# One ones-matmul for eight squares, and two float32 gate matmuls side by side, in a two-layer mLSTM / GLA trunk

## The chip, the cores and the metric

One Trainium2 chip, all 8 cores, each with one batch element and no exchange between cores. Engines are named as the profile names them: PE multiplies matrices (PEld is its loading of weights), DVE and POOL do elementwise work, ACT activation functions. PE writes its results into PSUM, which this kernel uses as a ring of banks: a bank is free again once another engine has read ("evicted") it. The metric is the device time of the slowest core in microseconds. A program on all cores has a second, slower state: in some executions one die or both run at a lower granted clock, the share of full speed at which PE is let run (here 1535 to 1802 us). A ratio is the mean time of one kernel's fast runs over that of the other's of the same rounds, so it is not quite the ratio of the medians quoted.

## The reference, cut to what matters

```python
def rmsnorm(x, g):                       # before each mixer, each MLP, and at the end
    y = x * lax.rsqrt(jnp.mean(x * x, axis=-1, keepdims=True) + EPS)
    return y * g
# layer 1 (GLA): low-rank gate, rank 16, 4 heads x 128
z = (z_low @ w_gate_up) + b_gate         # z_low: [S,16], w_gate_up: [16,512]
log_a = jax.nn.log_sigmoid(z) / 16.0     # then a running sum over the chunk
```

The rest (projections, chunkwise mixers, squared-ReLU MLPs) is large bf16 matmuls. mLSTM (a matrix memory) and GLA (gated linear attention) are the two layers' mixers, both worked out chunk by chunk.

## The kernel before

Activations lie transposed: features on partitions, 512 tokens (a group) along the free axis. A recording layer collects operations in source order and a list scheduler with estimated durations fixes each engine's order; the estimates (`ns=`) matter for nothing else. Names that return in the profiles: xT is the residual stream, xn its normalised copy, zl the rank-16 projection, sqb the summed squares, R the mixer's running state; wqk, wv, wo, wout, w1b and w2b are weights. The RMS statistics need a sum over 1024 features: ACT squares eight tiles, POOL adds them in two halves of four, and two matmuls with a matrix of ones sum the halves over the partitions.

```python
    def sq_half(g, hf):
        ks = [hf * 4 + i for i in range(4)]
        for i, k in enumerate(ks):
            act(sq[:, i % 2, :], xT[:, k, tgs(g)], AF.Square, ...)
            if i == 1:   tt(sd, sq[:, 0], sq[:, 1], ALU.add, ..., "pool")
            elif i == 2: tt(sd, sd, sq[:, 0], ALU.add, ..., "pool")
            elif i == 3: tt(sqb[:, hf, :], sd, sq[:, 1], ALU.add, ..., "pool")
    def sq_sum():
        a = nb()                                        # a PSUM bank of the ring
        for hf in range(2):
            mm(PB[a][:], ones_bf[:], sqb[:, hf, :], ...)
        rstd_fin(a)                                     # Ln, Exp on ACT through sd
```

In the GLA layer each group of tokens needs four gates, one for each head:

```python
        def zl_F(s, g):        # 8 matmuls, 16 output rows, then a copy to zl[0:16]
            ...
        def z_F(s, g, h):
            a, gp, p = nb(), g % 2, h % 2
            mm(PB[a][:], wgu[:, h * DK:(h + 1) * DK], zl[0:16, :], ..., 512, True)      # float32
            act(sd[:], PB[a][:], AF.Exp, ...)
            act(sd[:], sd[:], AF.Ln, ...)
            for c in range(4):                          # DVE: running sums, sd -> NB[p]
                tensor_tensor_scan(out=NB[:, p, chunk c], data0=ones_bf, data1=sd[:, chunk c], ...)
            act(EB[:, p, :], NB[:, p, :], AF.Exp, ..., scale=-1.0 / 16.0)
            act(NB[:, p, :], NB[:, p, :], AF.Exp, ..., scale=1.0 / 16.0)
            ...
```

(… marks cuts.)

## Time and profile before

| | before |
|---|---|
| median of the first 6 runs | 1519.9 us (1519.02 to 1573.5) |
| spans of the 8 cores, profiled run | 1512.3 to 1518.3 us |
| matmuls on PE | 7,554 (144 records are missing on two of the cores, the slowest among them) |
| PE busy / DVE / ACT / POOL | 96% / 53% / 40% / 12% |

A matmul's record lasts longer than the time after which the next may start, so durations of PE overlap. What counts is the distance between starts: 216 ns for 512 bf16 columns at the full clock. The lines themselves stand in the prediction.

### The profile page before, as it was taken

Reading aid. Unit: us, or ns where it says so; the run is one execution under the profiler, and the core shown is the slowest. Engines: PE = TensorE matmul, PEld = TensorE weight load, DVE = VectorE, ACT = ScalarE, POOL = GpSimd, SP = SyncE. Lnnn points to the kernel's source line nnn. Section 1 sums busy time; section 2 is a strip of 40 time slices with the busy share of each in tenths; the row PEclk is TensorE's granted clock in tenths of the full one; section 3 lists DMA queues with packets and bytes.
Section 4 is the critical chain, followed back from the end, with each engine's and each line's share of the span. In section 5 each row is a group of like instructions: output and inputs, shape, how many; then the busy total and the mean of one; then the engine's idle time right before and its main releaser. Section 6 shows DMA issues by size and latency. Waiting matters only on the chain.

```text
span 1518.3 us, 22604 instructions; the slowest of 8 cores (1512.3 to 1518.3 us)
## 1 busy us (share of the span) xinstructions
PE 1459.6 (96%) x7410; PEld 695.1 (46%) x7554; DVE 808.2 (53%) x1449; ACT 604.9 (40%) x1255; POOL 180.9 (12%) x170
## 2 busy tenths in 40 slices
PE   5999999899999999999999999999999999999996
PEld 1555455444444444444434544444444444444444
DVE  3187474865434434434656776769643343443467
ACT  3587676642022022033345776766310310301333
POOL 3012111330000000002010202024200000000042
PEclk9999999999999999999989999999999999999999
DMA  9840003633132033033001200037330231100014
GB/s 190 173 140 1 1 2 56 91 50 53 30 56 45 12 57 56 0 56 56 1 0 37 76 1 1 1 56 112 56 56 13 43 56 29 28 1 1 1 56 167
DMA packets 37378, 72.89 MB, mean 48 GB/s; under 512 B 4480, under 2 KB 6528, under 8 KB 37264
## 3 DMA queue, kind: packets, MB, share of 16 engines
q0 software_dynamic: 28640, 58.77, 21.4%
q1 hardware_dynamic: 8624, 12.66, 2.5%
q8 instruction: 63, 1.03, 0.3%
q14 instruction: 51, 0.42, 0.1%
HBM read 109.23 MB, written 8.39 MB: 77 GB/s over the span
## 4 chain that ended last, share of the span: by engine, by line
PE 86%; DVE 5%; issue 3%; DMA 2%; ACT 2%; POOL 1%; DVEq 0%; SPq 0%; ACTq 0%; POOLq 0%
PE ps L235 86%; DVE oT L249 1%; DVE R L249 1%; DVE xT L245 1%; DMA wqk<-m_win 1%; DMA xT<-xT 1%; DVE xn L249 1%; PE ps L749 1%; DMA wst<-m_wout 0%; POOL sd L245 0%; DVE hn L249 0%; ACT sq L241 0%; DVE ps L245 0%; POOL sqb L245 0%; ACT og L241 0%
## 5 line engine op out<-in xcount | busy, mean ns | idle before, releaser
L235 PE MATMUL ps<-xn,w1b 128*128 128x512 bf16 x2006 | 442.6, 379 | 2.8 <-DVE xT L245 0.5
L235 PE MATMUL ps<-hid,w2b 128*128 128x512 bf16 (+1 forms) x1948 | 415.7, 372 | 2.9 <-DVE xT L245 0.9
L241 ACT ACTIVATE rt<-ps 128x512 f32<-128x512 f32 x256 | 152.8, 597 | 606.2 <-PE ps L235 598.9
L245 DVE TENSOR_TENSOR xT<-ps,xT 128x512 f32<-128x512 f32 (+1 forms) x328 | 219.9, 675 | 250.3 <-PE ps L235 249.2
L235 PEld LDWEIGHTS ps<-xn,w1b 128*128 128x128 bf16 x2048 | 200.1, 98 | 241.6 <-issue 1.8
L235 PEld LDWEIGHTS ps<-hid,w2b 128*128 128x128 bf16 x1984 | 193.8, 98 | 222.2 <-issue 1.8
L245 DVE TENSOR_TENSOR hid<-rt 128x512 bf16<-128x512 f32 x240 | 170.1, 711 | 222.0 <-ACT rt L241 222.0
L241 ACT ACTIVATE sq<-xT 128x512 f32<-128x512 f32 (+2 forms) x168 | 97.3, 603 | 91.1 <-DVE xT L245 44.4
L235 PE MATMUL ps<-xn,wqk 128*128 128x512 bf16 x499 | 116.3, 384 | 6.9 <-DMA wqk<-m_win 6.2
L235 PE MATMUL ps<-wo,xn 128*128 128x512 bf16 x494 | 120.0, 386 | 1.7 <-DVE xT L245 0.6
L235 PE MATMUL ps<-wv,xn 128*128 128x512 bf16 x497 | 117.7, 383 | 1.1 <-DVE og L245 0.2
L235 PE MATMUL ps<-hnT,wout 128*128 128x512 bf16 x499 | 114.3, 379 | 1.3 <-ACT sd L241 0.6
L249 DVE SCALAR_TENSOR_TENSOR xn<-xT,gains,rstd 128x512 bf16<-128x512 f32 x128 | 99.9, 821 | 21.3 <-ACT rstd L241 21.3
L245 POOL TENSOR_TENSOR sd<-sq 128x512 f32<-128x512 f32 x34 | 44.2, 1300 | 516.1 <-ACT sq L241 323.7
L241 ACT ACTIVATE og<-og 128x512 f32<-128x512 f32 x128 | 80.5, 629 | 10.5 <-ACT og L241 0.4
L235 PEld LDWEIGHTS ps<-xn,wqk 128*128 128x128 bf16 x512 | 50.1, 99 | 65.6 <-issue 9.4
L235 PEld LDWEIGHTS ps<-wv,xn 128*128 128x128 bf16 x512 | 49.4, 99 | 60.8 <-issue 7.7
L235 PEld LDWEIGHTS ps<-wo,xn 128*128 128x128 bf16 x512 | 49.7, 99 | 54.4 <-issue 6.0
L235 PEld LDWEIGHTS ps<-hnT,wout 128*128 128x128 bf16 x512 | 48.6, 98 | 56.0 <-issue 2.8
L249 DVE SCALAR_TENSOR_TENSOR R<-R,egs,ps 128x256 f32<-128x256 f32 x120 | 57.3, 478 | 11.2 <-PE ps L235 4.2
L241 ACT ACTIVATE junk<-ps 128x256 bf16<-128x256 f32 x128 | 48.7, 380 | 14.7 <-PE ps L235 5.0
L245 POOL TENSOR_TENSOR sd<-sd,sq 128x512 f32<-128x512 f32 x34 | 44.8, 1317 | 71.2 <-ACT sq L241 70.9
(121 smaller groups left out, 991.1 us busy)
## 6 DMA issues: line engine op xcount, KB each, us to landing
w1b<-w POOLq DMA_DIRECT2D x16, 1024.0 KB, 15.0
w2b<-w POOLq DMA_DIRECT2D x16, 1024.0 KB, 12.2
outT<-oT SPq DMA_DIRECT2D x12, 512.0 KB, 2.9
xT<-xT POOLq DMA_DIRECT2D x2, 2048.0 KB, 29.0
wst<-m_wout POOLq DMA_DIRECT2D x4, 1024.0 KB, 6.5
wst<-g_wout POOLq DMA_DIRECT2D x4, 1024.0 KB, 5.3
xT<-xT SPq DMA_DIRECT2D x4, 512.0 KB, 6.6
xT<-xT SPq DMA_DIRECT2D x2, 1024.0 KB, 12.5
```

Of the source, the lines that this page charges most:

```text
L235: t.op("pe", lambda e: e.matmul(out, lhsT=lhsT, rhs=rhs, start=start, stop=stop), r=r, w=w, sig=sig, ns=max(cols, 150) * (1.7 if f32 else ...
L241: t.op("act", lambda e: e.activation(out=out, in_=in_, func=func, **kw), r=r, w=w, ns=190 + 0.84 * n + (190 if acc is not None else 0))
L245: t.op(eng, lambda e: e.tensor_tensor(out=out, in0=in0, in1=in1, op=op), r=r, w=w, ns=170 + 1.03 * n if eng == "dve" else 200 + 2.2 * n)
L249: t.op("dve", lambda e: e.scalar_tensor_tensor(out=out, in0=in0, scalar=scalar, in1=in1, op0=op0, op1=op1), r=r, w=w, ns=200 + 1.07 * n)
L749: t.op("pe", lambda e, h=h, e2=e2, e8=e8: e.transpose(tpS[:, e8, :], in_=hn[:, h, e2 * 128:(e2 + 1) * 128], identity=ident[:]), r=[("hn", ...
```

## The change

The intent is to take matmuls off the tensor engine. All eight squares are added on POOL before a single ones-matmul (in 14 of 17 sums; the three at the end, where the sum is waited for, keep two). And two heads' gates are computed by two matmuls in different 32-row groups of the array: a second copy of the low-rank projection (columns 32 to 47 of a widened `wz`, zeros between) puts `zl` on partitions 32 to 47 too, where the second head's weights lie.

```diff
     def sq_half(g, hf):
+        for i in range(4):
+            k = hf * 4 + i
+            act(sq[:, i % 2, :], xT[:, k, tgs(g)], AF.Square, ...)
+            if k == 5:
+                t.op("pool", ... sd = sd + sq[:, 0] ..., ns=0, more=True)
+                tt(sd[:], sd[:], sq[:, 1, :], ALU.add, ..., "pool")
+            ...
+            elif k == 7:
+                tt(sqb[:, 0, :], sd[:], sq[:, 1, :], ALU.add, ..., "pool")
...
-    wgu, _ = at("wgu", [16, 512], F32)
-    wz, _ = at("wz", [128, KC, 16], BF16)
+    wgu, _ = at("wgu", [48, 2, 128], F32)
+    wz, _ = at("wz", [128, KC, 48], BF16)
...
-        def z_F(s, g, h):
-            mm(PB[a][:], wgu[:, h * DK:(h + 1) * DK], zl[0:16, :], ...)
-            act(sd[:], PB[a][:], AF.Exp, ...)   # and Ln; scan sd -> NB
+        def z_F(s, g, hp):
+            gp, banks = g % 2, [nb(), nb()]
+            for p in range(2):
+                mm(PB[banks[p]][:], wgu[32 * p:32 * p + 16, hp, :], zl[32 * p:32 * p + 16, :], ...,
+                   True, True, p == 1, 256, True)
+            for p in range(2):                  # Exp, Ln, scans in place in NB[p]; EB, NB as before
...
-                return qk(0) + s.z(g + 1, 2) + o + qk(1) + s.z(g + 1, 3) + ops + qk(2) + v + qk(3)
+                return qk(0) + qk(1) + s.z(g + 1, 1) + o + ops + v + qk(2) + qk(3)
```

More of the change, by code (lines that the diff above doesn't have):

```diff
@@ L56, in ov, with op @@
         return r
-    def op(s, ename, fn, r=(), w=(), ns=200, sig=True):
+    def op(s, ename, fn, r=(), w=(), ns=200, sig=True, more=False):
         reads = [k for k in r if k[0] != "B"]
@@ L69, in op @@
         u["ns"] += ns
-        if sig:
+        if sig and not more:
             s.units.append(u)
@@ L403, in load_z @@
         n = 8 if layer == 0 else 16
-        t.dma("pool", [(wz[:, :, 0:n], src[:, :, 3072:3072 + n])], 500000, r=after, w=[("wz",)])
+        t.dma("pool", [(wz[:, :, c:c + n], src[:, :, 3072:3072 + n]) for c in ((0,) if layer == 0 else (0, 32))],
+              500000, r=after, w=[("wz",)])
     def load_w1(layer, q):
@@ L437, in sq_half, with sq_half2 @@
     def sq_half(g, hf):
+        for i in range(4):
+            k = hf * 4 + i
+            act(sq[:, i % 2, :], xT[:, k, tgs(g)], AF.Square, [("xT", k, g)], [("sq", i % 2)], 512)
+            if k == 5:
+                t.op("pool", lambda e: e.tensor_tensor(out=sd[:], in0=sd[:], in1=sq[:, 0, :], op=ALU.add),
+                     r=[("sd",), ("sq", 0)], w=[("sd",)], ns=0, more=True)
+                tt(sd[:], sd[:], sq[:, 1, :], ALU.add, [("sd",), ("sq", 1)], [("sd",)], 512, "pool")
+            elif i == 1:
+                tt(sd[:], sq[:, 0, :], sq[:, 1, :], ALU.add, [("sq", 0), ("sq", 1)], [("sd",)], 512, "pool")
+            elif i == 2:
+                tt(sd[:], sd[:], sq[:, 0, :], ALU.add, [("sd",), ("sq", 0)], [("sd",)], 512, "pool")
+            elif k == 3:
+                tt(sd[:], sd[:], sq[:, 1, :], ALU.add, [("sd",), ("sq", 1)], [("sd",), ("sqb", 0)], 512, "pool")
+            elif k == 7:
+                tt(sqb[:, 0, :], sd[:], sq[:, 1, :], ALU.add, [("sd",), ("sq", 1)], [("sqb", 1)], 512, "pool")
+    def sq_half2(g, hf):
         ks = [hf * 4 + i for i in range(4)]
@@ L450, in rstd_fin, with sq_sum @@
         act(rstd[:], sd[:], AF.Exp, [("sd",)], [("rstd",)], 512, scale=-0.5)
-    def sq_sum():
+    def sq_sum(two=False):
         a = nb()
-        for hf in range(2):
-            mm(PB[a][:], ones_bf[:], sqb[:, hf, :], [("sqb", hf), ("ones_bf",)], [("B", a)], hf == 0, hf == 1,
-               hf == 1, 512)
+        if two:
+            for hf in range(2):
+                mm(PB[a][:], ones_bf[:], sqb[:, hf, :], [("sqb", hf), ("ones_bf",)], [("B", a)], hf == 0, hf == 1,
+                   hf == 1, 512)
+        else:
+            mm(PB[a][:], ones_bf[:], sqb[:, 0, :], [("sqb", 0), ("sqb", 1), ("ones_bf",)], [("B", a)], True, True,
+               True, 1024)
         rstd_fin(a)
@@ L600, in zl_F @@
             for k in range(KC):
-                mm(PB[a][0:16, :], wz[:, k, 0:16], XN[:, x, k, :], [("wz",), ("xn", x, k)], [("B", a)],
+                mm(PB[a][0:48, :], wz[:, k, :], XN[:, x, k, :], [("wz",), ("xn", x, k)], [("B", a)],
                    k == 0, k == KC - 1, k == KC - 1, 512)
-            t.op("dve", lambda e: e.tensor_copy(out=zl[0:16, :], in_=PB[a][0:16, :]), r=[("B", a)], w=[("zl",)],
+            t.op("dve", lambda e: e.tensor_copy(out=zl[0:48, :], in_=PB[a][0:48, :]), r=[("B", a)], w=[("zl",)],
@@ L604, in zl_F @@
                  ns=670)
-        def z_F(s, g, h):
-            a, gp, p = nb(), g % 2, h % 2
-            mm(PB[a][:], wgu[:, h * DK:(h + 1) * DK], zl[0:16, :], [("wgu",), ("zl",)], [("B", a)], True, True, True,
-               512, True)
-            act(sd[:], PB[a][:], AF.Exp, [("B", a), ("ngbg",)], [("sd",)], 580, scale=-1.0, bias=ngbg[:, h:h + 1])
-            act(sd[:], sd[:], AF.Ln, [("sd",)], [("sd",)], 512, bias=1.0)
-            for c in range(4):
-                t.op("dve", lambda e, c=c: e.tensor_tensor_scan(
-                    out=NB[:, p, c * CH:(c + 1) * CH], data0=ones_bf[:], data1=sd[:, c * CH:(c + 1) * CH],
-                    initial=0.0, op0=ALU.mult, op1=ALU.add), r=[("ones_bf",), ("sd",)], w=[("NB", p)], ns=425)
-            act(EB[:, p, :], NB[:, p, :], AF.Exp, [("NB", p)], [("EB", p)], 512, scale=-1.0 / 16.0)
-            act(NB[:, p, :], NB[:, p, :], AF.Exp, [("NB", p)], [("NB", p)], 512, scale=1.0 / 16.0)
-            t.op("dve", lambda e: e.tensor_copy(
-                out=egs[:, gp, h * 4:(h + 1) * 4],
-                in_=EB[:, p, :].rearrange("p (c n) -> p c n", n=CH)[:, :, CH - 1]),
-                r=[("EB", p)], w=[("egs", gp)], ns=170)
+        def z_F(s, g, hp):
+            gp, banks = g % 2, [nb(), nb()]
+            for p in range(2):
+                mm(PB[banks[p]][:], wgu[32 * p:32 * p + 16, hp, :], zl[32 * p:32 * p + 16, :], [("wgu",), ("zl",)],
+                   [("B", banks[p])], True, True, p == 1, 256, True)
+            for p in range(2):
+                h, a = hp * 2 + p, banks[p]
+                nbv, nk = NB[:, p, :], ("NB", p)
+                act(nbv, PB[a][:], AF.Exp, [("B", a), ("ngbg",)], [nk], 580, scale=-1.0, bias=ngbg[:, h:h + 1])
+                act(nbv, nbv, AF.Ln, [nk], [nk], 512, bias=1.0)
+                for c in range(4):
+                    cv = NB[:, p, c * CH:(c + 1) * CH]
+                    t.op("dve", lambda e, cv=cv: e.tensor_tensor_scan(
+                        out=cv, data0=ones_bf[:], data1=cv, initial=0.0, op0=ALU.mult, op1=ALU.add),
+                        r=[("ones_bf",), nk], w=[nk], ns=425)
+                act(EB[:, p, :], nbv, AF.Exp, [nk], [("EB", p)], 512, scale=-1.0 / 16.0)
+                act(nbv, nbv, AF.Exp, [nk], [nk], 512, scale=1.0 / 16.0)
+                t.op("dve", lambda e, h=h, p=p: e.tensor_copy(
+                    out=egs[:, gp, h * 4:(h + 1) * 4],
+                    in_=EB[:, p, :].rearrange("p (c n) -> p c n", n=CH)[:, :, CH - 1]),
+                    r=[("EB", p)], w=[("egs", gp)], ns=170)
@@ L764, in op_, with z @@
             return [lambda j=j: s.op_F(g, j) for j in range(KC)]
-        def z(s, g, h):
-            return [] if s.m else [lambda: s.z_F(g, h)]
+        def z(s, g, hp):
+            return [] if s.m else [lambda: s.z_F(g, hp)]
         def gate_slots(s, g):
@@ L788, in fills @@
                         return o + qk(3)
-                    return x[:2] + o + qk(0) + s.z(1, 2) + x[2:] + qk(1) + s.z(1, 3) + v
+                    return x[:2] + o + qk(0) + qk(1) + s.z(1, 1) + x[2:] + v
                 if c == 2:
@@ L814, in run @@
                                 addx(0, fn)
-                            for h in range(2):
-                                for fn in s.z(1, h):
-                                    addx(2, fn)
+                            for fn in s.z(1, 0):
+                                addx(2, fn)
                     elif c == 0:
@@ L826, in run @@
                             addx(n, fn)
-                        for h in range(2):
-                            for fn in s.z(g + 1, h):
-                                addx(4 + h, fn)
+                        for fn in s.z(g + 1, 0):
+                            addx(4, fn)
                 for n, fn in hooks.get(i, []):
@@ L870, in build @@
     t.dma("sp", [(ong[:], ong_d)], 1000, w=[("ong",)])
-    t.dma("sp", [(wgu[:], g_wgu_d)], 1000, w=[("wgu",)])
+    wgu_v = g_wgu_d.rearrange("r (a b n) -> r b a n", b=2, n=128)
+    t.dma("sp", [(wgu[32 * b:32 * b + 16, :, :], wgu_v[:, b]) for b in range(2)], 1000, w=[("wgu",)])
     t.dma("sp", [(gbg[:], g_bg_d)], 1000, w=[("gbg",)])
     t.op("dve", lambda e: e.memset(ones_bf[:], 1.0), w=[("ones_bf",)])
+    t.op("dve", lambda e: e.memset(wz[:], 0.0), w=[("wz",)])
     t.op("dve", lambda e: e.memset(ident[:], 0.0), w=[("ident",)])
@@ L1027, in build @@
     dn[2][0]()
+    dn[2][1]()
     m1.zl_F(0)
-    dn[2][1]()
+    dn[2][2]()
     m1.z_F(0, 0)
-    m1.z_F(0, 1)
-    dn[2][2]()
     dn[2][3]()
@@ L1036, in build @@
             fn()
-        if h < 2:
-            m1.z_F(0, 2 + h)
-            dn[2][4 + 2 * h]()
-            dn[2][5 + 2 * h]()
+        if h == 1:
+            m1.z_F(0, 1)
+            for j in range(4, 8):
+                dn[2][j]()
     for fn in m1.v(0):
@@ L1074, in build @@
             if j in (4, 7):
-                sq_half(g, j // 7)
+                sq_half2(g, j // 7)
             if gen is not None and j >= 3:
                 next(gen, None)
-        sq_sum()
+        sq_sum(True)
         gen = out_ops(g, 0, GS)
```

## The prediction

> **What bounds the kernel now.** I read the page of the slowest core first: the busy shares, the chain that ended last, the row of the granted clock. Then the waits of the tensor engine, then the two groups of matmuls that the change touches, and last their neighbourhood in the timeline.
>
> ```profile
> PE 1459.6 (96%) x7410; PEld 695.1 (46%) x7554; DVE 808.2 (53%) x1449; ACT 604.9 (40%) x1255; POOL 180.9 (12%) x170
> ...
> PE 86%; DVE 5%; issue 3%; DMA 2%; ACT 2%; POOL 1%; DVEq 0%; SPq 0%; ACTq 0%; POOLq 0%
> ```
>
> PE is busy 96% of the span and is 86% of the chain. A busy PE is not a PE at its peak, so I looked at what it waits for:
>
> ```profile
> PE ps L235 <- ACT sq L241: 16.4, 9, 8.7
> PE ps L235 <- DMA wqk<-m_win: 6.2, 1, 6.2
> PE ps L235 <- DVE R L249: 5.6, 10, 1.8
> ...
> PE ps L235 <- ACT sd L241: 0.6, 1, 0.6
> PE ps L235 <- POOL sqb L245: 0.4, 1, 0.4
> ```
>
> About 44 us in all. The first 16.4 us lie in the start-up statistics and in the last half group (both keep their code) and 6.2 us in the first weight load. The two producers in question, POOL's sqb and the statistics' Ln (sd), keep PE for 1.0 us. So almost anywhere in the two places that change, PE time taken away is time taken off the end, and PE time saved does not fall behind another wait. The question is how much PE time goes.
>
> ```profile
> L235 PE MATMUL ps<-zl,wgu 16*128 16x512 f32 x32 | 19.1, 691 | 0.0
> ...
> L235 PE MATMUL ps<-sqb,ones_bf 128*128 128x512 bf16 x33 | 10.4, 378 | 1.0 <-POOL sqb L245 0.4 <-DVE xT L245 0.4
> L245 POOL TENSOR_TENSOR sd<-sq 128x512 f32<-128x512 f32 x34 | 44.2, 1300 | 516.1 <-ACT sq L241 323.7
> ```
>
> 16 float32 gate matmuls stand as 32 records: each is two passes. The durations overlap, so I don't use them; I use distances between starts. Here is one gate matmul between two bf16 streams, and one sum of squares:
>
> ```profile
> 751.02 0.81 PE L235 MATMUL ps<-xn,wqk 128*128 128x512 bf16 x3
> 751.76 1.12 PE L235 MATMUL ps<-zl,wgu 16*128 16x512 f32 x2
> 752.82 0.61 PE L235 MATMUL ps<-xn,w2b 128*128 128x512 bf16 x2
> ...
> 774.65 0.59 PE L235 MATMUL ps<-sqb,ones_bf 128*128 128x512 bf16 x2
> ```
>
> In the single records the last bf16 matmul starts 309 ns before the gate (216 between bf16 matmuls, so 93 to get in), the two passes are 535 ns apart, and the next bf16 matmul starts 518 ns after the second: 93 + 1053 = 1146 ns for one gate. Two gates back to back (at 736.48) have passes 429 ns apart and take 93 + 1912 = 2005 ns. The two sqb matmuls are 216 ns apart.
>
> One place is odd:
>
> ```profile
> 780.00:800.00 20.00, 16.92 (x41) 5.29 (x40) 11.96 (x24) 6.22 (x12) 0.00 (x0) 0.66 0.00 0
> ```
>
> Between 780 and 800 us the granted clock is 0.66: the zl matmuls come one by one behind DVE's xn, 663 ns apart, and from 787 us all matmuls take double time for some 10 us. A gate pair falls into it and takes 3710 ns in place of 1912.
>
> **What the Trainium skill says.** "TensorE: Matmul & The Clock Gate", Single matmul / Back-to-back issue gap: a warm 512-column matmul costs 512/2.4 + 2.5, about 216 ns; this trace has 215 and 216. The same page, Part 3 (Packing small matmuls): a matmul with few contraction rows costs as much as one with 128; matmuls in different 32-row groups run at once, four of them measured 3.07 times as fast; but matmuls start and end strictly in program order, only weight loads are pulled ahead. The trace of before has only one row group in use, so it can't show the overlap; that 16 rows cost no less than 128 it does show (429 ns a pass, at float32's half rate). "TensorEngine Tiling (Array Packing)", Key Properties: a change of tiling mode drains the engine; the 93 ns into a gate and some 90 ns after its last pass (518 against 429) agree. "GPSIMD Engine Reference", section 3: a two-input elementwise op is about twice as slow as on VectorE; here 1.27 us against 0.68.
>
> **The change, part by part.**
>
> (1) Sum of squares. Of 17 sums, 14 go from two ones-matmuls to one; the three of the tail keep two. PE saves 14 x 0.216 = 3.0 us. POOL gets 7 adds a sum for 6: 14 x 1.27 = 18 us more on an engine that is 12% busy. Does the sum land later? In the second half POOL now can start when the first new square is there, and does four adds; before, it waited for two squares and did three. At 121 us, the tightest case (PE takes the sum 0.1 us before its record ends), the halves go: half one ends 121.07, square 4 is ready at 121.14, so four adds from 121.24 with no buffer wait end near 126.4; before they ended at 126.87. At 306 us the same working gives about 310 in place of 311.49, because square 4 had been ready at 300.75. Of the 14, ten have 3 us or more of slack. So the extra add costs nothing or almost nothing: 0 to 0.5 us.
>
> (2) The gates. 16 single gate matmuls become 8 pairs; the second of a pair has its weights and its zl on partitions 32 to 47, so it sits in another row group. Before, on PE: 14 runs (12 singles, two doubles, one of these cold). From the single records, start to start less 216 for the bf16 matmul ahead, they sum to 19.6 us. For a pair the program order is A pass 1, A pass 2, B pass 1, B pass 2. If order is strict and a pass must wait for the pass in its own row group, only A2 and B1 overlap: three pass times, not four and not two: 93 + 535 + 429 + 520 = 1577 ns. Seven warm pairs are 11.0 us; the one in the cold stretch was 4055 with its entry, less one cold pass of 854, 3.2 us. Sum 14.2, saving 19.6 - 14.2 = 5.4 us.
>
> (3) zl. 48 stationary columns in place of 16, 512 moving columns either way: 8 matmuls of 216 ns four times, no change; the copy to zl works on 48 partitions in the same 0.67 us. The zeros between are a memset at the start, before PE begins. The second 16-column load at 538 us puts about 0.9 us more of issue on POOL ahead of weights that are used 200 us later: hidden.
>
> (4) Exp, Ln and scan now work in place in NB, not through the one sd. The second head's Exp no longer waits for the first head's scan; the work is the same. In exchange each pair needs two PSUM banks at once of a ring of four, and both EB and NB buffers free, so the queries and keys of two heads are projected ahead of it. PE's order shows 16 to 32 other matmuls between a pair and the projections that need it, at least 7 us, against about 7 us for the pair's chain (0.69 + 0.63 + 2.0 + 1.3, the second head some 2 us later). I book 0, with 2 us either way, and another 2 us for the scheduler's other reorderings.
>
> Sum: 3.0 + 5.4 = 8.4 us off, 1519.9 - 8.4 = about **1511.5 us**, 0.55%.
>
> **The rivals.**
>
> A: full overlap, both gates in the time of one. Pair 1146 ns, seven are 8.0, the cold one about 2.35: 10.4, saving 9.2, time about 1507.5. For it: the skill's 3.07 for four tiles. Against it: that is for single-pass tiles; here the two passes of A stand together in the order.
>
> C: no overlap (the float32 passes exclude one another). Pair 2005 ns, 14.0 + 4.06 = 18.1, saving 1.5 only, from fewer entries; time about 1515.5. Nothing in this trace speaks against it.
>
> D: a new wait takes it back: PE at the ones-matmul for POOL's later sum, or PE for banks held by the gates' Exp. In the worst case four tight sums lose 1.3 us each and eight pairs 0.5 us: about 9 us, so a time as before, 1520. Slacks and the working in (1) speak against.
>
> E: the cold stretch at 787 us goes, or another comes. It is worth some 5 us at half speed plus about 4 us of waits. The order of zl, wo and the pair there is the same as before and the xn ops still pace it, so I expect it to stay; it is present on six of eight cores before.
>
> **Range and chances.** I weigh the overlap of two passes 0.5, full overlap 0.25, none 0.25; with reordering of 3 us and the cores' own spread (1512.3 to 1518.3) the range is **1504.5 to 1517.5**. 2% is 30 us; the whole work removed or at stake is 10 to 15 us, so: faster by over 2% 0.01, within 2% 0.98, slower by over 2% 0.01.
>
> **What would show it.** Ones-matmuls of sqb: 20 in place of 34, each 216 ns. Start to start from the bf16 matmul before a gate pair to the one after it, less 216: 1.58 us if two passes overlap, 1.15 if all do, 2.0 if none. The second and third pass of a pair starting within 20 ns of each other would be the overlap itself. Waits of PE for sqb and for sd stay under 2 us; POOL's busy time rises by 18 us. I am wrong if PE waits for sqb or for the gates' Exp by several us, if the chunk after a pair waits for EB or NB, or if the clock of 0.66 near 790 us is gone or has a twin elsewhere.

## The result, and the profile after

| | before | after |
|---|---|---|
| time | 1519.9 us (first session) | 1509.6 us, median of 8 runs, two of them slow (1784 us) |
| ratio of fast runs | | 0.9926, interval 0.9914 to 0.9938 |
| spans of the cores, profiled run | 1512.3 to 1518.3 us | 1500.6 to 1508.7 us |

The ratio is 11.2 us of 1519.9, where 8.4 had been forecast. The first line of the page of the kernel after (busy us, share, instructions of each engine):

```profile
PE 1446.2 (96%) x7396; PEld 691.5 (46%) x7540; DVE 810.4 (54%) x1450; ACT 604.8 (40%) x1255; POOL 199.9 (13%) x185
```

Its waits of PE, from the list of waits (total us, times, longest):

```profile
PE ps L235 <- DVE R L249: 5.5, 10, 1.1
...
PE ps L235 <- DVE xT L245: 4.6, 6, 1.3
...
PE ps L235 <- ACT ktok L241: 1.3, 1, 1.3
PE ps L235 <- POOL sqb L245: 0.8, 2, 0.6
```

PE holds 14 matmuls fewer and is 13.4 us less busy; POOL is 19.0 us busier. PE still hardly waits for the sum (0.8 us), but it waits for DVE's xT, the eviction of a PSUM bank, 4.6 us where it had been 2.4 (these are the slowest cores, core 0 before and core 6 after). Next the groups of instructions that the change touches:

```profile
L235 PE MATMUL ps<-xn,wz 128*48 128x512 bf16 x32 | 9.4, 400 | 2.2 <-DVE xn L249 2.1
L235 PE MATMUL ps<-zl,wgu 16*128 16x512 f32 x32 | 9.2, 654 | 0.0
...
L235 PE MATMUL ps<-sqb,ones_bf 128*128 128x512 bf16 x19 | 7.3, 391 | 1.4 <-POOL sqb L245 0.8 <-DVE xT L245 0.4
```

And one gate pair in the timeline of PE (start, duration, instruction, count):

```profile
745.50 0.38 PE L235 MATMUL ps<-xn,wqk 128*128 128x512 bf16 x1
745.81 1.13 PE L235 MATMUL ps<-zl,wgu 16*128 16x512 f32 x4
746.87 0.60 PE L235 MATMUL ps<-xn,w2b 128*128 128x512 bf16 x2
```

The reader sees 32 gate records as before, but 9.2 us of busy time for 19.1, and four of them between 745.81 and 746.87: two gates now take the 1.06 us that one took. 48 output rows cost zl next to nothing: eight zl matmuls that follow one another take 1.53 us from first to last start for 1.51 (the 9.4 us for 9.1 of busy time are durations, which also depend on the clock). The single records of this pair start at 0, 7, 533 and 540 ns.

To see where the time went, I added up the distances between starts of PE's records, core by core, and split them: the gates (from the bf16 matmul ahead to the one after, less 216 ns), the ones-matmuls of sqb, idle time of PE (without its longest wait, some 9 us for the first squares at the start; so the column is below the 43.5 us that the list of waits of before adds up to), and what 512-column bf16 matmuls spaced 400 to 450 ns take above 216 (half clock). Means of the six cores whose trace has all records, in us:

| kernel | span | gates | sums | PE waits | half clock | all else |
|---|---|---|---|---|---|---|
| before | 1514.2 | 19.1 | 8.3 | 31.6 | 5.7 | 1449.5 |
| after | 1504.7 | 9.7 | 4.9 | 35.4 | 4.9 | 1449.8 |
| difference | -9.5 | -9.4 | -3.4 | +3.8 | -0.8 | +0.3 |

So the change saves 12.8 us of PE's work and gives 3.8 back as waits, all of it in the second layer (7.9 to 11.6). These are one execution's mean cores; the slowest core, which the times measure, gained 9.6 in these two executions and 11 over the runs.

### The profile page after: what moved, and what is told of

Same layout as the page of the kernel before. It is cut to its first block, busy times and chain, and to the rows that moved or that the text cites. A ratio compares the mean times of both kernels' runs of the same rounds, so it can differ in the third digit from the quotient of the medians.

```text
span 1508.7 us, 22612 instructions; the slowest of 8 cores (1500.6 to 1508.7 us)
## 1 busy us (share of the span) xinstructions
PE 1446.2 (96%) x7396; PEld 691.5 (46%) x7540; DVE 810.4 (54%) x1450; ACT 604.8 (40%) x1255; POOL 199.9 (13%) x185
## 4 chain that ended last, share of the span: by engine, by line
PE 85%; DVE 7%; issue 3%; DMA 2%; ACT 2%; POOL 0%; DVEq 0%; SPq 0%; ACTq 0%; POOLq 0%
PE ps L235 84%; DVE xn L249 1%; DVE oT L249 1%; DVE R L249 1%; DMA xT<-xT 1%; DVE xT L245 1%; DMA wqk<-m_win 1%; DVE hn L249 1%; PE ps L777 1%; DMA wst<-m_wout 0%; PE ps L666 0%; DVE ps L245 0%; DMA wst<-g_wout 0%; DVE NB L641 0%; ACT og L241 0%
## 5 line engine op out<-in xcount | busy, mean ns | idle before, releaser
L245 POOL TENSOR_TENSOR sd<-sd,sq 128x512 f32<-128x512 f32 x62 | 81.2, 1310 | 73.2 <-ACT sq L241 66.7
L245 POOL TENSOR_TENSOR sd<-sq 128x512 f32<-128x512 f32 x20 | 25.9, 1295 | 466.3 <-ACT sq L241 441.0
```

Of the source, the lines that this page charges most:

```text
L245: t.op(eng, lambda e: e.tensor_tensor(out=out, in0=in0, in1=in1, op=op), r=r, w=w, ns=170 + 1.03 * n if eng == "dve" else 200 + 2.2 * n)
```

## The experiments

Theory: the pairing pays through overlap of *both* float32 passes, and the sum through the matmuls left out; some of it comes back as waits that the new order makes. Rivals: the overlap is only partial and the order or the clock brought the rest; POOL's longer sum is waited for. Eleven runs were made, nine of edited kernels and two repeats (e_after, e_late_again), all correct. The table has their split, in the columns of above.

| kernel | median, us | ratio to before, interval | gates | sums | PE waits | half clock |
|---|---|---|---|---|---|---|
| e_sq | 1516.3 | 0.9968, 0.9955 to 0.9981 | 18.4 | 4.9 | 32.1 | 4.8 |
| e_gates | 1512.2 | 0.9947, 0.9933 to 0.9960 | 9.9 | 8.5 | 34.3 | 4.3 |
| e_same_rows | 1520.2 | 0.9996, 0.9982 to 1.0009 | 17.3 | 4.9 | 37.0 | 5.4 |
| e_sig | fast runs 1509.4, 1510.1 | 0.9935, 0.9907 to 0.9962 | 9.7 | 4.9 | 35.2 | 3.7 |
| e_quad | 1512.7 | 0.9952, 0.9924 to 0.9979 | 6.0 | 4.9 | 38.1 | 6.1 |
| e_pool8 | 1519.1 | 0.9992, 0.9970 to 1.0015 | 10.4 | 4.7 | 43.2 | 6.0 |
| e_split | 1518.9 | 0.9984, 0.9971 to 0.9998 | 11.3 | 5.1 | 39.0 | 7.7 |
| e_late | 1503.3 | 0.9891, 0.9870 to 0.9912 | 9.3 | 5.0 | 33.6 | 2.9 |
| e_before_late | 1511.3 | 0.9938, 0.9918 to 0.9958 | 17.6 | 8.3 | 29.6 | 3.4 |
| e_after | 1510.7 | 0.9935, 0.9915 to 0.9956 | 9.6 | 5.0 | 36.5 | 4.9 |
| e_late_again | fast runs 1502.7 to 1503.1 | 0.9887, 0.9864 to 0.9910 | 9.2 | 4.9 | 33.9 | 2.3 |

Each ratio is against runs of the kernel before on the same chip. Medians can hold slow runs; the ratios don't.

### e_sq: the sums alone

The kernel before with the new `sq_half` and `sq_sum`, nothing else.

> The kernel before with the sum-of-squares part alone (14 of 17 sums with one ones-matmul, seven adds on POOL). Theory: PE time saved goes straight to the end and the extra add lies in slack, so 14 x 0.216 = 3.0 us plus a few tenths of transitions: 1516.2 to 1517, ratio about 0.998. PE waits for sqb under 1.5 us in all, POOL busy +18 us. Rival: POOL's later sum is waited for at the four tight sums and gives 1 to 3 us back: 1517.5 to 1520.

Measured: 0.9968, 4.9 us, with an interval of 2.9 to 6.8. The sums take 3.4 us less on PE (14 matmuls, 0.24 us each with their transitions), and waits rise by only 0.5. The theory stands; the 1 us or so above it lies in the half-clock column (-0.9), which varies from run to run, and inside the interval. With e_gates below, the two parts alone sum to 13.0 us where both together gave 11.2; the intervals are wide enough for that.

### e_gates: the pairing alone, with names

```diff
-    wgu, _ = at("wgu", [48, 2, 128], F32)
+    wgu, WG = at("wgu", [48, 2, 128], F32)
+    wguB, _ = at("wguB", [48, 2, 128], F32, WG)        # same place, a name of its own
...
-                mm(PB[banks[p]][:], wgu[32 * p:32 * p + 16, hp, :], ...)
+                mm(PB[banks[p]][:], (wguB if p else wgu)[32 * p:32 * p + 16, hp, :], ...)
```

> The gate pairing alone on the kernel before (sums of squares as before), with the second head's weights under a name of their own (wguB, same place) so that records of the two matmuls can be told apart. Theory: both float32 passes of the second head overlap those of the first, i.e. its first pass overtakes the first head's second pass: records in the order wgu, wguB, wgu, wguB, 7 ns apart within each couple, PE 9.5 us less for gates, some 3.5 us more waits of PE in the second layer: 1512 to 1514.5, ratio about 0.9955. Rival (program order kept): order wgu, wgu, wguB, wguB with only the middle two together; the trace of after speaks against it by its spacing, the names decide.

Measured: 0.9947, 8.1 us. The timeline of PE in this run names the two matmuls:

```profile
746.21 0.69 PE L235 MATMUL ps<-zl,wgu 16*128 16x512 f32 x1
746.22 0.69 PE L235 MATMUL ps<-zl,wguB 16*128 16x512 f32 x1
746.75 0.59 PE L235 MATMUL ps<-zl,wgu 16*128 16x512 f32 x1
746.75 0.59 PE L235 MATMUL ps<-zl,wguB 16*128 16x512 f32 x1
```

The compiled program lists, for a pair, first head's pass 1 and pass 2, then second head's pass 1 and pass 2 (read, with the row-group masks, in the compiled instruction stream of the changed kernel, and in that of e_gates itself; no trace shows it). On the chip the second head's pass 1 starts before the first head's pass 2: it overtakes it by half a microsecond. The partial overlap, which keeps program order, is ruled out.

### e_same_rows: the same order without the second row group

```diff
-    wgu, _ = at("wgu", [48, 2, 128], F32)
+    wgu, _ = at("wgu", [16, 2, 2, 128], F32)
...
-                mm(PB[banks[p]][:], wgu[32 * p:32 * p + 16, hp, :], zl[32 * p:32 * p + 16, :], ...)
+                mm(PB[banks[p]][:], wgu[0:16, p, hp, :], zl[0:16, :], ...)
```

zl has 16 columns again. The order of matmuls on PE is that of the changed kernel, row by row.

> The changed kernel with both heads of a pair on partitions 0 to 15 (same row group, 16 columns for zl), the order of all instructions on every engine unchanged. Theory: the overlap is what the pairing buys, so a pair goes from 1.15 back to about 2.0 us on PE: 8 x 0.85 = 6.8 us longer than the changed kernel, about 1515.5 us, ratio to before about 0.9970. zl costs the same with 16 as with 48 columns. Rival (the gain comes from the new order or from fewer entries into float32): within 2 us of the changed kernel, about 1509 to 1511.

Measured: 0.9996, so all of the gain is gone. Here is a pair in its timeline:

```profile
746.30 1.98 PE L235 MATMUL ps<-zl,wgu 16*128 16x512 f32 x4
748.21 0.39 PE L235 MATMUL ps<-xn,w2b 128*128 128x512 bf16 x1
```

1.91 us for two gates where the changed kernel takes 1.06. The gates column gives 7.6 us back against the 6.8 expected (the pair in the half-clock stretch is dearer: 4.1 us on five of the eight cores), and waits rise by 1.6. By the ratios it is 10.6 us slower than the changed kernel, more than the theory said. It also shows what the new order is worth without overlap: the gates save 1.8 us from fewer entries into float32, the waits cost 5.4 more than before, so by these columns pairing without overlap would have been a loss that only the sums' 3.4 us made good. This run holds the order fixed and takes away the second row group: it is what shows that the overlap, and not the order, brings the gain.

### e_sig: who signals

A semaphore update on both matmuls of a pair, not on the second alone.

> The changed kernel with a semaphore update on each gate matmul of a pair, not on the second alone. Theory: the overlap does not depend on who signals: the records stay couples 7 ns apart and the first head's Exp starts no later; 1508 to 1510 us, as the changed kernel. Rival (an update on the first head's last pass makes the second head wait): pairs at 1.6 to 2.0 us, 3.5 to 7 us longer.

Measured: 0.9935 on two fast runs; pairs of 1.15 us, gates 9.7 us. The overlap does not hang on a single update. With two fast runs the time says no more than "as the changed kernel".

### e_quad: four row groups

```diff
+                banks = [nb() for _ in range(4)]
+                for h in range(4):
+                    mm(PB[banks[h]][:], wgu[32 * h:32 * h + 16, :], zl[32 * h:32 * h + 16, :], ...)
+                for h in range(4):        # Exp to NB[0], NB[1], sd, sq[1]; the rest of heads 2, 3 later
```

> The changed kernel with all four heads of a group in four row groups (112 columns for zl, four banks at once; the Exp of heads 2 and 3 parked in two idle tiles until the second half). Theory: passes of all row groups run together, so the eight records of a quad start as two couples of four, and four heads take about 1.15 us of PE where two pairs take 2.3: 4 x 1.15 = 4.6 us less for gates; but PE finds its four banks held until the first Exp, some 0.7 us each time, so 1505 to 1508 us. Rival (only two row groups overlap, or a pass can overtake no more than one other): gates cost as in pairs, and with the bank waits the time is 1509 to 1513.

The timeline of PE, with the matmul that follows:

```profile
889.61 1.14 PE L235 MATMUL ps<-zl,wgu 16*128 16x512 f32 x8
890.68 0.28 PE L235 MATMUL ps<-vt,ktok 128*128 128x256 bf16 x1
```

Four gates, eight passes, in 1.07 us; single records start at 0, 7, 14, 20 and 534, 540, 547, 554 ns. So four row groups overlap too, and a pass overtakes as many as three others. The gates drop to 6.0 us. But PE waits 2.7 us more, 0.9 of that right around the gates (in the first quad the fourth bank came free so late that its matmul ran alone, the quad taking 3.1 us), and a wait for the gates' Exp (NB) stands in its list that the changed kernel's list does not have:

```profile
PE ps L235 <- ACT NB L241: 2.5, 3, 1.1
```

The clock column is 1.2 us worse, and the time is 1512.7 us. By these columns gain and loss cancel (0.2 us of loss), while the mean core is 2.3 us slower; some 2 us are in no column. So the 3.7 us saved do not reach the time; whether e_quad is slower than the changed kernel is not shown, since the intervals of their ratios overlap. That four banks held at once take most of it is likely (the waits for NB are of that size) but not separated from the order. A miss by time, a hit by mechanism.

### e_pool8: one more add on POOL

An eighth add, unused, ahead of the last one of each of the 14 sums.

> The changed kernel with one more add on POOL ahead of the last one of each of the 14 sums (its result is not used): the sum lands 1.27 us later. Theory: ten of the 14 sums have over 1.5 us of slack, so at most four are waited for: 0 to 4 us longer, 1508.5 to 1513. Rival (POOL's sum is on the path everywhere): 14 x 1.27 = 18 us longer.

Measured: 0.9992, some 10 us slower than the changed kernel, well above the 4 us allowed. The waits of PE in this run:

```profile
PE ps L235 <- POOL sqb L245: 5.4, 4, 1.9
```

Four waits in place of two, and 4.6 us more. In the changed kernel four of the 14 sums land less than 0.6 us before PE takes them, and those four are the ones waited for here. The rest is not waiting for the sum itself: other waits rise by 3.2, the half-clock and gate columns by 1.1 and 0.7, though the order of the matmuls on PE is that of the changed kernel, one for one. I can't say more on that part than where it stands; its cause is open. Even so, POOL is 13% busy, and 1.27 us more a sum still cost 10 us, about half of it at four sums. The seventh add was nearly free because POOL starts each second half one square earlier: at the first sum its fourth add begins at 122.28 us, 0.22 us after the third, where it had stood idle for 0.93 us:

```profile
122.28 1.27 POOL L443 TENSOR_TENSOR sd<-sd,sq 128x512 f32<-128x512 f32 x1 [0.22 <-ACT sq L241]
```

The same place before:

```profile
122.00 1.26 POOL L245 TENSOR_TENSOR sd<-sq 128x512 f32<-128x512 f32 x1 [0.93 <-ACT sq L241]
```

The eighth finds no such idle time left there: the adds that follow are 0.20 us apart.

### e_split: the second head's scans later

The new wait of 1.3 us near 755 us stands in the changed kernel's timeline of PE (the bracket holds the idle time ahead and who ended it):

```profile
755.23 2.10 PE L235 MATMUL ps<-xn,wqk 128*128 128x512 bf16 x9 [1.28 <-DVE xT L245]
```

And DVE in the microseconds before it:

```profile
748.55 3.93 DVE L641 TENSOR_TENSOR_SCAN NB<-ones_bf,NB 128x128 f32<-128x128 bf16 x6 [1.88 <-ACT NB L241]
752.40 0.15 DVE L646 COPY egs<-EB 128x4 f32<-128x4 f32 x1
752.59 1.91 DVE L641 TENSOR_TENSOR_SCAN NB<-ones_bf,NB 128x128 f32<-128x128 bf16 x2
754.42 1.26 DVE L245 TENSOR_TENSOR xT<-ps,xT 128x512 f32<-128x512 f32 x2
```

With two heads' gates ready at once DVE runs eight scans, six of them in a row, while PE's next matmul waits for DVE's xT, which evicts a down-projection result from PSUM. That all banks are full then is my reading of that wait. The edit records the second head's scans one or two slots later (and tells the scheduler 500 ns for a scan, not 425).

> The changed kernel with the second head's four scans and two Exp recorded one or two slots later, so that DVE can drain PSUM between the two heads' scans. Theory: the new waits of PE in the second layer (1.3 us at about 755 us, for DVE's xT while DVE runs eight scans and PSUM banks are full) come from the eight scans standing together; waits of PE there drop by 1 to 3 us and the time with them: 1506 to 1508, ratio 0.991 to 0.992. Rival: the waits come from elsewhere in the new order and move rather than go: 1508 to 1511.

Measured: 0.9984, 1518.9 us; a miss. The wait at 755 us is gone, as the timeline of this run shows (wqk after w2b again, though earlier, and no bracket):

```profile
752.22 5.99 PE L235 MATMUL ps<-xn,wqk 128*128 128x512 bf16 x27
```

But the waits of PE, listed for the stretch from 1000 to 1060 us, now hold one of 2.9 us:

```profile
PE ps L235 <- DVE R L249: 2.9, 1, 2.9
```

Waits are 3.6 us more than in the changed kernel, the half clock 2.8 and the gates 1.6. The rival holds: the scheduler, which also had a new estimate for a scan, moved what comes after the edit, and the waits moved with it. That the eight scans delay the xT that PE waits for at 755 us is seen in the trace, and the wait went when they were spread; since the order of PE changed too, that is no clean proof. That spreading them pays is not shown.

### e_late, e_late_again and e_before_late: the stretch of half clock

The prediction had noted a stretch at about 787 us in which zl runs at DVE's pace and the clock then halves. In the trace of before the granted clock there is 0.5 for 13.7 us on six cores and for 6.8 us on two, in that of after for 6.8 us on seven and 10.2 us on one. The edit records xn, zl and the gates of that chunk over later slots, so that PE has other work meanwhile:

```diff
-                            for fn in ([] if s.m else st + xs + gs):
-                                addx(0, fn)
-                            for fn in s.z(1, 0):
-                                addx(2, fn)
+                            for n, fn in ([] if s.m else list(zip((0, 0, 0, 1, 2, 3, 4, 5), st + xs + gs))):
+                                addx(n, fn)
+                            for fn in s.z(1, 0):
+                                addx(6, fn)
```

> The changed kernel with the second layer's first zl and its pair recorded later in their chunk (xn spread over four slots, zl at slot 5, pair at slot 6), so that PE has other matmuls while DVE makes xn. Theory: the stretch of lower clock near 785 us comes from PE running zl at DVE's pace (0.66 us a matmul); without it 3.5 us of waits and 2 to 4 us of matmuls at half speed go: 1502 to 1506 us, and few matmuls of 430 ns between 740 and 1000 us. Rival (the waits move to other places in the chunk): 1507 to 1511.

Measured: 0.9891, 1503.3 us. A window of the changed kernel, 780 to 800 us (busy us and instructions of PE, PEld, DVE, ACT and POOL, then the granted clock, DMA share, GB/s):

```profile
780.00:800.00 20.00, 17.14 (x72) 7.07 (x73) 14.17 (x29) 10.47 (x22) 0.00 (x0) 0.83 0.01 1
```

The same stretch of the program in e_late, 775 to 795 us:

```profile
775.00:795.00 20.00, 19.49 (x105) 9.24 (x103) 18.29 (x39) 12.13 (x27) 0.00 (x0) 1.00 0.00 1
```

105 matmuls in 20 us in place of 72, at the full clock. The second zl group takes 2.4 us in place of 5.8, and the low clock near 785 us is gone on all eight cores.

> The kernel before with only the later zl, xn and gates of the second layer's first chunk, as in e_late. Theory: the stretch of lower clock is a fault of its own, there before the change, and what its removal gives (on e_late: 2.5 us of waits, 1.6 us of matmuls at half speed, half a us in the gates, some 2 us elsewhere) it gives here too, with more in the gates because a pair in that stretch costs 1.8 us more: 1512 to 1515 us, ratio 0.995 to 0.997. Rival: it only helps with paired gates: 1518 to 1521.

> The changed kernel once more, unedited, beside e_late on one chip. Expected: ratio to before between 0.991 and 0.994 again, about 1509 us.

> e_late once more beside the changed kernel. Theory: it stays 5 to 6 us ahead of the changed kernel, ratio to before 0.988 to 0.990, about 1503 us. Rival (its three fast runs were lucky): within 2 us of the changed kernel.

The kernel before with this edit alone (its gates at the same slots) ran at 0.9938, 9.4 us faster, more than the 5 to 8 expected. The same window of that run (the kernel before has 0.66 at 780 to 800 us, in the prediction):

```profile
775.00:795.00 20.00, 19.36 (x102) 9.22 (x102) 18.03 (x37) 11.54 (x32) 0.00 (x0) 1.00 0.00 1
```

So the stretch was a fault of its own, there before the change, and the edit that removes it is worth almost as much as the whole change. Of the mean core's 8.4 us, 2.4 stand under half clock, 2.0 under waits and 1.5 under gates; 2.6 are in no column. How much is the clock and how much the waits for xn that the edit also removes, no run separates. The changed kernel again gave 0.9935, and e_late 0.9887, some 7 us ahead of it on the same chip. e_late is the fastest kernel here.

## Why the prediction was right or wrong, point by point

- **What bounds the kernel.** Right. PE's time removed came off the end: with all the split's columns added, the mean core's 9.5 us are explained but for 0.3.
- **(1) Sums.** Right in mechanism and size: 3.4 us on PE for 3.0 (the difference is the transitions), POOL 19.0 us busier for 18, PE's wait for the sum 0.8 us. The working of the tightest sum, at 121 us, was wrong: it put the four adds end to end, 126.4 us in place of 126.87, but an add that needs the one before starts 0.20 us after that one's end, in the trace of before too. Counted from the end of the first half, the sum lands 5.9 us later, for 5.8 before: no gain. And a sum at about 1030 us that had 5.5 us of slack before has 0.14 us now. That PE waits only 0.8 us is thus partly luck; e_pool8 shows how thin the slack is.
- **(2) Gates: this is the step that failed.** "If order is strict and a pass must wait for the pass in its own row group, only A2 and B1 overlap: three pass times" put 5.4 us on the gates. They saved 9.4: rival A, full overlap, 9.2 predicted. The second premise holds (same-row passes follow each other 429 ns apart in e_same_rows); the first does not: the second head's pass overtakes. What stood against A was the order of the passes in the program, and that is what the chip did not keep.
- **(3) zl.** Right: 9.4 us for 9.1 with 48 output rows.
- **(4) Order and buffers.** Booked 0 with 2 us either way; the waits of PE rose by 3.8 us. The working had compared the pair's chain with the matmuls before its users, and that held: PE waits 0.3 us for qT. What it left out is whom DVE keeps waiting meanwhile: 1.3 us of the new waits follow the eight scans, which delay an eviction (xT). Another new wait of 1.3 us, for ACT's ktok, was not traced. e_same_rows shows these waits without any overlap (5.4 us above before, of which the sums explain 0.5 by e_sq), so most of them belong to the order.
- **The sum.** The two errors have opposite signs (4.0 us too little saved, 3.8 us of waits not booked), so 1511.5 against 1509.6 is partly luck: the measured time lies in the range, and the gain of 11.2 us is a third above the 8.4 forecast.
- **Rival E.** The stretch stayed, as expected, with some 0.8 us less at half clock. (Before, it was there on all eight cores, shorter on two; the prediction had counted six.) The edit of e_before_late, which removes it, gave 9.4 us where the stretch had been put at 5 + 4; the total fits, its two parts are not measured one by one.

## What to carry to other kernels

Here two float32 matmuls with 16 contraction rows took the time of one once the second had its own 32-row group. Read the distances between starts, not the durations, to see such an overlap; the program's order did not have to be interleaved for it. Then look at what the pair's results ask of the engines behind it at one moment, banks, evictions and in-order queues, for that is where a third of this gain went. And before trimming matmuls, look at the row of the granted clock: a few microseconds of matmuls at another engine's pace and the clock that followed cost here almost as much as the whole change brought.

## What the Trainium skill lacked or had wrong

- "TensorE: Matmul & The Clock Gate", Part 3, says that matmuls start and end strictly in program order. For float32 matmuls in different row groups they don't: program order wgu, wgu, wguB, wguB ran as wgu, wguB, wgu, wguB, 7 ns apart within a couple and 527 ns from couple to couple (e_gates); with four row groups a pass overtook three (e_quad). Its advice that a signal on the last matmul is enough was followed and gave correct results; e_sig, with both signalling, was correct too.
- No page gives the time of a float32 matmul ("FP8 and Floating Point Precision" counts four passes for true FP32 and leaves it at that). The traces show two records 429 ns apart at 512 columns, together 3.97 times the 216 ns of bf16, overlapping across two or four row groups (two gates 1.06 us, four 1.07 us), with 93 ns to get in and 91 ns to get out (520 against 429).
- "TensorE: Matmul & The Clock Gate", Part 1, has the clock halve after idle windows and return after about 3.4 us of activity. PE was not idle here: in the profiled run of before it ran one matmul every 0.66 us, a third of what it can do, and 2.8 to 3.9 us after the first of them the granted clock fell to 0.5, for 6.8 us on two cores and for 13.7 us on the others. The page does tell of short idles between groups of matmuls that lower the clock (psum-queue depth-cycling); what it lacks is a figure for how sparse the matmuls may be.
